# Four more stretches of a hand-written order of instructions (around steps 21–31, 99–104, 127–132 and 160–170 of a decoder layer)

## The chip, the cores and the metric

The kernel runs on one core of one Trainium2 chip. The metric is the device time of one execution in microseconds (us); the time before is 1079.78 us, the median of three runs (1078.62, 1079.78, 1080.32).

## The reference, cut to what matters

One layer on 512 tokens of width 1024, everything in float32: a SwiGLU feed-forward block (inner width 2816), a mixing block (chunked gMLP gating beside a Mamba-2 scan), a second SwiGLU block, a gated embedding and a last RMSNorm.

```python
h = h + 0.5 * swiglu(rmsnorm(h, ffn1_norm[i]), ffn1_w_gate[i], ffn1_w_up[i], ffn1_w_down[i])
n = rmsnorm(h, mix_norm[i])
proj = n @ w_in[i]
u, v, z, xbc, dt_raw = jnp.split(proj, IN_SPLITS, axis=-1)
ya = chunked_spatial_gating(gelu(u), gelu(v), gm_ln_g[i], gm_ln_b[i], gm_w_s[i], gm_b_s[i])   # layernorm of v inside
ya = rmsnorm(ya, gm_out_norm[i])
yb = mamba2_mixer(z, xbc, dt_raw, ...)
h = h + jnp.concatenate([ya, yb], axis=-1) @ w_out[i]
h = h + 0.5 * swiglu(rmsnorm(h, ffn2_norm[i]), ffn2_w_gate[i], ffn2_w_up[i], ffn2_w_down[i])
h = h + sigmoid(rmsnorm(h, ple_norm[i]) @ ple_w_gate[i] + ple_b_gate[i]) * (p[i] @ ple_w_proj[i])
return rmsnorm(h, final_norm)
```

## The kernel before

Every float32 operand of a large product is split into a high part that TensorE can take (`hi`, a cast on ScalarE) and the rest (`lo`, a subtraction on VectorE), and three products are added in PSUM (hi·hi, hi·lo, lo·hi). So every block of weights of 128 x 1024 that arrives by DMA (tile `raw`, `rawb`, `rawd` or `s`) needs one cast (L511, tiles `whi` or `whix`) and one subtraction (L515, tiles `wlo` or `wlox`) before TensorE can use it. `whi` and `wlo` have three buffers each, `whix` and `wlox` one each.

The program is a list of 251 **steps**: 0–99 the embedding product and the first feed-forward block, 100–136 the mixing block, 137–152 the output projection, 153–250 the second feed-forward block. A step has one product on TensorE and pieces around it: `load` (the DMA), `cast` and `split` (L511, L515), `after` (what reads the finished product), `post` and `rest` (more of the same). In the feed-forward blocks a group of 256 inner columns takes seven products (seven instead of eight, by Strassen's scheme, L725; tiles `mm` and `a` in PSUM, inputs `xfa` and `xfb`), and "down" steps (L235, tile `sm`) stand in between; their result is added to the residual `h` by L930. The gate `g` of a group is put together on VectorE (L867, L872, L878, L883), passed through silu on ScalarE (L874) and split again (L894 `ghi`, L896 `glo`).

At the end of the first block the residual tiles are finished two by two (L930), split for the mixing block (L210 on ScalarE and L211 on VectorE, both write tiles `x`) and squared (L277 on ScalarE, tile `tmp`), and GpSimd adds up the squares (L278). In the mixing block, per pair of heads, L1497 and L1461 on VectorE prepare what the scan's products L1471 and L1478 read, L1488 and L1489 take them up, and GpSimd goes on with L1490 and L1491. The layernorm of `v` stands there too: `v_moments` (four `bn_stats`, L1598), `v_factor` (four `bn_aggr`, L1602, and the eleven small instructions of `rsqrt`, L244 to L249) and `v_normed` (L1607). `spatial` sums a weight matrix by a product with ones (L1565), whose two inputs are the tiles `convin`: a cast (L202) and a subtraction (L203). L1569 uses the sum.

The order of the instructions is written out, not found by a scheduler: inside `tc.manual_schedule` TensorE, ScalarE, VectorE and the sync engine's DMA queue take their instructions in the order in which the program makes them. `run` first lists all pieces of all steps in a standing order as generators (`tasks`), each of which yields between its instructions. Then it walks the string `ENTRY`: `split26` runs all that is left of a piece, `split26:1` runs it up to its first yield. What the string does not name follows in the standing order.

```python
for entry in order.split():
    name, _, count = entry.partition(":")
    for _ in islice(tasks[name], int(count) if count else None):
        pass
for task in tasks.values():
    for _ in task:
        pass
```

Of the kernel before, what the change touches and what calls it, by code (L numbers as in the profile page):

```python
# [57 lines left out]
split10 split10.1 load15 product9 split11 after8 load16 product10 after9 split12 load17 after10  # L58
after10.1:1 product11 after11 split13 split14:1 after10.1 split14 product12 after+10 after11.1
after11.2 after12:1 product13 after+11 split15 after13:1 split16 after13:1 after12 product14  # L60
after13
"""

BUFS = {
# [35 lines left out]
def layer_kernel(ctx: ExitStack, tc: tile.TileContext, a: dict, out: bass.AP):  # L100
# [22 lines left out]
    def open_region(side, name):  # L123
        close_region(side)
        names[side] = name
        region[side] = tc.alloc_tile_pool(name=name, bufs=1, side=side, reuse_waits="tile")
        if side == "left":
            pad(region[side], name)
# [279 lines left out]
    def run(steps, opened, order):  # L408

        n = len(steps)  # L410
        held, tasks = [], {}

        def pieces(fn):
            got = fn()
            if isinstance(got, GeneratorType):
                yield from got
            yield

        def do(i, what, which=0):
            if 0 <= i < n:  # L420
                fns = getattr(steps[i], what)
                if what == "after":
                    fns = fns[which] if len(fns) > which else ()
                for k, fn in enumerate(fns if isinstance(fns, (list, tuple)) else [fn for fn in (fns,) if fn]):
                    tasks[f"{what}{'+' * which}{i}" + (f".{k}" if k else "")] = pieces(fn)

        loaded = 0
        for i in range(-3, n + 2):
            while loaded < n and loaded - steps[loaded].lead <= max(i, -1):
                if steps[loaded].from_right and any(i <= k < loaded for k in opened):  # L430
                    held.append(loaded)
                else:
                    do(loaded, "load")
                loaded += 1
            do(i, "product")
            if i in opened:
                tasks[f"open{i}"] = pieces(lambda i=i: open_region("right", opened[i]))
                while held:
                    do(held.pop(0), "load")
            late = 0 <= i - 1 < n and not steps[i - 1].urgent  # L440
            do(i + 2, "cast")
            do(i - 2, "after", 1)
            for what in ("split", "after") if late else ("after", "split"):
                if what == "split":
                    do(i + 2, "split")
                    do(i + 3, "sums")
                else:
                    do(i - 1, "after")
            do(i - 1, "post")
            do(i, "rest")  # L450
        for entry in order.split():
            name, _, count = entry.partition(":")
            for _ in islice(tasks[name], int(count) if count else None):
                pass
# [3 lines that stand above are left out]
# [1278 lines left out]
    with tc.manual_schedule(engines=ORDERED):  # L1736
        run(sum(parts, []) + steps, {ends[0]: "mix_right", ends[2]: "ffn2_right"}, ENTRY)
# [193 lines left out]
```

## Time and profile before

| what | value |
|---|---|
| runs | 1078.62, 1079.78, 1080.32 us |
| the profiled execution | 1078.85 us, of which the profiled span is 1077.1 us |
| TensorE (PE) busy | 1065.2 us, 99% of the span; weight loads (PEld) 992.3 us, 92% |
| VectorE (DVE) busy | 780.1 us, 72% |
| ScalarE (ACT) busy | 514.8 us, 48% |
| GpSimd (POOL) busy | 136.2 us, 13% |
| mean granted TensorE clock | 0.998 |

Times in rows of the profile are microseconds from the start of the span. A row of the timeline gives start, duration, engine, line, operation, names (out<-in), shapes and how many instructions were merged; in brackets stands the idle time of the engine before it and what ended it. Matmuls are pipelined: a row lists a matmul of 256 columns with 0.28 us, but they start 0.113 us apart when nothing is late (24 in 2.72 us), and those of 512 columns 0.227 us. So a wait of TensorE is read here from start to start. The chain of waits is followed back from the last instruction; its rows give start, length, engine, tile, line and count.

### The profile page before, as it was taken

The numbers are of one execution on the slowest core, as the hardware profiler recorded it, in microseconds if no ns is written. First come the engines' busy times: TensorE is split into PE (matmuls) and PEld (weight loads), VectorE is DVE, ScalarE is ACT, GpSimd is POOL, SyncE is SP. The second block draws the span as 40 slices with busy tenths as digits, with TensorE's granted clock in tenths as the row PEclk, the third lists the DMA queues.
The fourth block names the chain that finished last, engine by engine and source line by source line (L and its number), as shares of the span: only waits on it lengthen the run. The fifth ranks groups of instructions, "written<-read, shape, count | busy, mean of one in ns | idle before, by whom it ended". The sixth has DMA issues, their size and how long they took to land.

```text
span 1077.1 us, 18907 instructions
## 1 busy us (share of the span) xinstructions
PE 1065.2 (99%) x7850; PEld 992.3 (92%) x7850; DVE 780.1 (72%) x1081; ACT 514.8 (48%) x711; POOL 136.2 (13%) x125
## 2 busy tenths in 40 slices
PE   9999999999999999999999999999999999999997
PEld 8999999999999888787888888999999999999996
DVE  7987676666666686766997756688766676677766
ACT  6744444343444455575754334354444434343554
POOL 0100000000001201043233000000000000000311
PEclk9999999999999999999999999999999999999999
DMA  9986776665523232444432223667756676633412
GB/s 343 303 226 193 191 192 180 174 184 156 134 60 127 90 98 81 146 131 135 131 105 79 98 98 117 202 162 204 212 142 172 182 195 178 179 115 111 144 41 79
DMA packets 50038, 163.91 MB, mean 152 GB/s; under 512 B 5664, under 2 KB 6176, under 8 KB 49952
## 3 DMA queue, kind: packets, MB, share of 16 engines
q1 hardware_dynamic: 40016, 129.09, 34.4%
q0 software_dynamic: 8640, 31.46, 16.4%
q10 hardware_dynamic: 1296, 2.16, 0.6%
q8 instruction: 61, 1.00, 0.4%
q14 instruction: 25, 0.20, 0.1%
HBM read 158.43 MB, written 4.26 MB: 151 GB/s over the span
## 4 chain that ended last, share of the span: by engine, by line
PE 90%; DVE 4%; DMA 2%; ACT 2%; issue 1%; SPq 0%; DVEq 0%; ACTq 0%
PE sm L235 24%; PE mm L725 20%; PE a L725 15%; PE mm L219 6%; PE sm L219 6%; PE mm L235 6%; PE a L219 5%; PE a L235 3%; PE sm L814 2%; DMA whix<-in_x_rows 1%; PE mm L814 1%; PE a L814 1%; DVE wlo L515 1%; DMA raw<-in_ffn_gu 1%; PE sm L288 1%
## 5 line engine op out<-in xcount | busy, mean ns | idle before, releaser
L511 ACT CAST whi<-raw 128x1024 fp32r<-128x1024 f32 x138 | 144.3, 1046 | 160.6 <-issue 61.0
L515 DVE TENSOR_TENSOR wlo<-raw,whi 128x1024 fp32r<-128x1024 f32 x137 | 172.0, 1255 | 62.4 <-ACT whi L511 60.8
L725 PE MATMUL mm<-xfb,whi 128*128 128x256 f32 x960 | 166.2, 276 | 0.0
L235 PE MATMUL sm<-ghi,wlox 128*128 128x256 f32 x592 | 150.9, 277 | 0.3 <-DVE wlox L515 0.3
L235 PE MATMUL sm<-glo,whix 128*128 128x256 f32 (+1 forms) x512 | 151.1, 295 | 0.0
L235 PE MATMUL sm<-ghi,whix 128*128 128x256 f32 (+1 forms) x512 | 150.3, 294 | 0.0
L725 PEld LDWEIGHTS mm<-xfb,whi 128*128 128x128 f32 x960 | 144.6, 188 | 0.0
L725 PE MATMUL mm<-xfb,wlo 128*128 128x256 f32 x480 | 132.5, 276 | 0.0
L235 PEld LDWEIGHTS sm<-ghi,wlox 128*128 128x128 f32 x592 | 111.1, 188 | 7.5 <-DVE wlox L515 0.7
L725 PE MATMUL a<-xfb,whi 128*128 128x256 f32 x640 | 111.0, 276 | 0.0
L725 PEld LDWEIGHTS a<-xfb,whi 128*128 128x128 f32 x640 | 96.4, 188 | 0.2 <-issue 0.2
L235 PEld LDWEIGHTS sm<-ghi,whix 128*128 128x128 f32 x512 | 96.1, 188 | 0.0
L235 PEld LDWEIGHTS sm<-glo,whix 128*128 128x128 f32 x512 | 96.1, 188 | 0.0
L725 PEld LDWEIGHTS mm<-xfb,wlo 128*128 128x128 f32 x480 | 90.1, 188 | 0.0
L725 PE MATMUL a<-xfb,wlo 128*128 128x256 f32 x320 | 88.5, 276 | 0.0
L515 DVE TENSOR_TENSOR wlox<-rawd,whix 128x1024 fp32r<-128x1024 f32 (+1 forms) x40 | 45.7, 1142 | 58.2 <-ACT whix L511 58.2
L515 DVE TENSOR_TENSOR wlo<-rawb,whi 128x1024 fp32r<-128x1024 f32 x52 | 63.6, 1223 | 18.8 <-ACT whi L511 18.8
L874 ACT ACTIVATE g<-g 128x512 f32<-128x512 f32 x40 | 25.3, 632 | 106.8 <-DVE g L872 106.8
L740 POOL DMA_DIRECT2D raw<-in_ffn_gu x20 | 17.3, 866 | 418.0 <-DVE h L930 195.4
L511 ACT CAST whi<-rawb 128x1024 fp32r<-128x1024 f32 x52 | 54.3, 1044 | 27.2 <-DVE rawb L735 17.8
L930 DVE SCALAR_TENSOR_TENSOR h<-sm,h 128x512 f32<-128x512 f32 x96 | 63.2, 684 | 3.3 <-PE sm L235 3.2
L219 PE MATMUL sm<-x,whi 128*128 128x512 f32 x208 | 65.5, 396 | 0.0
(403 smaller groups left out, 2490.3 us busy)
## 6 DMA issues: line engine op xcount, KB each, us to landing
raw<-in_ffn_gu SPq DMA_DIRECT2D x56, 512.0 KB, 6.2
rawd<-in_ffn_down SPq DMA_DIRECT2D x40, 512.0 KB, 4.2
rawb<-in_ffn_gu SPq DMA_DIRECT2D x32, 512.0 KB, 5.6
raw<-in_ffn_gu POOLq DMA_DIRECT2D x30, 512.0 KB, 5.3
raw<-in_w_in SPq DMA_DIRECT2D x29, 512.0 KB, 3.5
s<-in_ffn_gu SPq DMA_DIRECT2D x20, 512.0 KB, 7.1
s<-in_ffn_gu POOLq DMA_DIRECT2D x20, 512.0 KB, 8.4
raw<-in_w_out SPq DMA_DIRECT2D x16, 512.0 KB, 3.4
```

Of the source, the lines that this page charges most:

```text
L219: nc.tensor.matmul(ps, w, x, start=first and n == 0, stop=last and n == 2, skip_group_check=True)
L235: nc.tensor.matmul(ps[:, tok], wt[:, c], xt[:, tok], start=first and k == i == 0, stop=last and k == len(xs) - 1 and i == len(by_part) - 1 ...
L288: nc.tensor.matmul(ps[:, c : c + 1], part[:, c * P : (c + 1) * P], ones[:, 0:1], start=part is t, stop=part is not t or more is None,)
L511: nc.scalar.copy(self.hi[:, : self.n], self.raw[:, : self.n])
L515: nc.vector.tensor_tensor(self.lo[:, :n], self.raw[:, :n], self.hi[:, :n].bitcast(F32), ALU.subtract)
L725: nc.tensor.matmul(o, wt[:, c], xt, start=fresh and p == m == n == 0, stop=last and n == 2, skip_group_check=True,)
L740: nc.gpsimd.dma_start(w21.raw, self.src[0], accum_op=ALU.add)
L814: nc.tensor.matmul(by_half(ps)[:, s], (whi, whi, wlo)[n][:, c], t[:, s, n % 2], start=not lower and p == i == 0, stop=lower and p == len(s ...
L874: nc.scalar.activation(t, t, AF.Silu)
L930: nc.vector.scalar_tensor_tensor(h[d], ps[d], 0.5, h[d], ALU.mult, ALU.add)
```

## The change

The string `ENTRY` gets more entries, and `run` a rule for them: `..after23` runs all pieces that stand ahead of `after23` in the standing order. Nothing else changes; the lines of the kernel after move by 11 in the head of the file and by 18 behind `run`.

```diff
-after13
+after13 ..after23 split26:1 after23:2 split26 after23 ..product99 after98:1 product99 open99
+cast101 after+97 split101 after98 after+98 after98 load104 product100 cast102 ..load131 load131
+after126.3 load131 product127 cast129 after126 after126.1 after126.2 after126.3 split129 post126
...
         for entry in order.split():
+            if entry.startswith(".."):
+                for name, task in tasks.items():
+                    if name == entry[2:]:
+                        break
+                    for _ in task:
+                        pass
+                continue
             name, _, count = entry.partition(":")
```

TensorE, GpSimd and the sync engine's queue keep their order word for word. VectorE and ScalarE have the same instructions in another order at five points. Two of them are small. In step 23's `after` the cast and subtraction of a down step's weights (`whix` on ScalarE, `wlox` on VectorE) come to stand ahead of the cast and subtraction of the gate (`ghi`, `glo`); before they stood behind them. And in step 126's `after` the four `bn_stats` of `v` come to stand ahead of L1497 and the two L1461 on VectorE, not behind them. The other three are shown by their instructions.

**The start of the mixing block (steps 99 to 102).** On ScalarE, the program before has there (`whi` of `raw_4036` is the cast for step 102, `tmp` are squares of the residual, `x` the split residual):

```order
L511 CAST whi_4156<-raw_3973 128x1024
L277 ACTIVATE tmp_4159<-h_96 128x512
L277 ACTIVATE tmp_4162<-h_100 128x512
L210 ACTIVATE x_4168<-h_97,vec_70 128x512
L210 ACTIVATE x_4172<-h_101,vec_70 128x512
L511 CAST whi_4197<-raw_4036 128x1024
L277 ACTIVATE tmp_4200<-h_97 128x512
L277 ACTIVATE tmp_4203<-h_101 128x512
L210 ACTIVATE x_4209<-h_98,vec_70 128x512
```

and the changed one, same engine, same place:

```order
L529 CAST whi_4157<-raw_3973 128x1024
L288 ACTIVATE tmp_4160<-h_96 128x512
L288 ACTIVATE tmp_4163<-h_100 128x512
L221 ACTIVATE x_4168<-h_97,vec_70 128x512
L221 ACTIVATE x_4172<-h_101,vec_70 128x512
L288 ACTIVATE tmp_4176<-h_97 128x512
L288 ACTIVATE tmp_4179<-h_101 128x512
L529 CAST whi_4203<-raw_4036 128x1024
L221 ACTIVATE x_4209<-h_98,vec_70 128x512
```

The cast for step 102 moved behind the two squares. On VectorE, at the same place, one residual sum (`h_97`) moved ahead of the subtraction for step 101; before:

```order
L211 SCALAR_TENSOR_TENSOR x_4100<-h_100,vec_70,x_4099 128x512
L515 TENSOR_TENSOR wlo_4157<-raw_3973,whi_4156 128x1024
L930 SCALAR_TENSOR_TENSOR h_97<-sm_4038,h_97 128x512
L930 SCALAR_TENSOR_TENSOR h_101<-sm_4061,h_101 128x512
L211 SCALAR_TENSOR_TENSOR x_4169<-h_97,vec_70,x_4168 128x512
```

and now:

```order
L222 SCALAR_TENSOR_TENSOR x_4100<-h_100,vec_70,x_4099 128x512
L948 SCALAR_TENSOR_TENSOR h_97<-sm_4038,h_97 128x512
L533 TENSOR_TENSOR wlo_4158<-raw_3973,whi_4157 128x1024
L948 SCALAR_TENSOR_TENSOR h_101<-sm_4061,h_101 128x512
L222 SCALAR_TENSOR_TENSOR x_4169<-h_97,vec_70,x_4168 128x512
```

So `h_97` no longer stands behind a subtraction that needs the cast of step 101.

**The layernorm of `v` (steps 129 and 130).** On VectorE, before; `convin_5887` is the second input of the product L1565 behind step 130, and `v_factor` begins with the first BN_AGGR:

```order
L1489 TENSOR_TENSOR u_5637<-u_5637,a_818_5834 128x384
L203 TENSOR_TENSOR convin_5887<-xs_5783,convin_5886 128x512
L1632 TENSOR_TENSOR u_5900<-mm_5789,rall_4343 128x512
L515 TENSOR_TENSOR wlo_5880<-raw_5725,whi_5879 128x1024
L1569 SCALAR_TENSOR_TENSOR xs_5699<-sm_5849,vec_70,xs_5699 128x128 x4
L1602 BN_AGGR vstat_120<-bnst_5163 128x2
```

and in the changed program:

```order
L1507 TENSOR_TENSOR u_5637<-u_5637,a_818_5834 128x384
L1620 BN_AGGR vstat_120<-bnst_5163 128x2
...
L255 TENSOR_SCALAR nv_5890<-vstat_120 128x4
L256 TENSOR_SCALAR ny_5891<-nv_5890 128x4
L258 TENSOR_TENSOR nt_5892<-ny_5891 128x4
...
L260 SCALAR_TENSOR_TENSOR vr_121<-nt_5892,ny_5891 128x4
L214 TENSOR_TENSOR convin_5905<-xs_5783,convin_5904 128x512
L1650 TENSOR_TENSOR u_5918<-mm_5789,rall_4343 128x512
```

The whole of `v_factor`, fifteen instructions, now stands directly behind L1489 (L1507 there), and `convin`, L1632, `wlo` and the four L1569 follow it.

**The start of the second feed-forward block (steps 160 to 170).** On VectorE before; `wlo_7459` belongs to the last product of group 1, `wlo_7487` and `wlo_7520` to the first two of group 2, `wlox_7559` to a down step and `wlo_7592` to the third product of group 2:

```order
L515 TENSOR_TENSOR wlo_7459<-rawb_6944,whi_7458 128x1024
L930 SCALAR_TENSOR_TENSOR h_95<-sm_7402,h_95 128x512
L930 SCALAR_TENSOR_TENSOR h_99<-sm_7413,h_99 128x512
L515 TENSOR_TENSOR wlo_7487<-raw_1052_7332,whi_7486 128x1024
L867 TENSOR_TENSOR g_7429<-a_1038_7217,p_1048_7313 128x512
...
L930 SCALAR_TENSOR_TENSOR h_100<-sm_7475,h_100 128x512
L883 TENSOR_TENSOR g_7429<-g_7429,a_1038_7217 128x512
L896 TENSOR_TENSOR glo_7555<-g_7429,ghi_7554 128x1024
L515 TENSOR_TENSOR wlox_7559<-rawd_7400,whix_7558 128x512
L735 TENSOR_TENSOR raw_1052_7332<-raw_1052_7332,s_1056_7365 128x1024
L515 TENSOR_TENSOR wlo_7592<-raw_1052_7332,whi_7591 128x1024
```

and now:

```order
L948 SCALAR_TENSOR_TENSOR h_95<-sm_7402,h_95 128x512
L948 SCALAR_TENSOR_TENSOR h_99<-sm_7413,h_99 128x512
L885 TENSOR_TENSOR g_7429<-a_1038_7217,p_1048_7313 128x512
L533 TENSOR_TENSOR wlo_7487<-raw_1052_7332,whi_7486 128x1024
...
L753 TENSOR_TENSOR raw_1052_7332<-raw_1052_7332,s_1058_7368 128x1024
L901 TENSOR_TENSOR g_7429<-g_7429,a_1038_7217 128x512
L533 TENSOR_TENSOR wlox_7527<-rawd_7400,whix_7526 128x512
L948 SCALAR_TENSOR_TENSOR h_100<-sm_7475,h_100 128x512
L533 TENSOR_TENSOR wlo_7532<-raw_1052_7332,whi_7531 128x1024
L914 TENSOR_TENSOR glo_7564<-g_7429,ghi_7563 128x1024
```

The reading of `a` (L867) moved ahead of a subtraction, and the sum of two weight blocks (L735, L753 in the changed file) with the subtraction that follows from it moved ahead of the gate's `glo`. On ScalarE the casts moved in the same way: that of `s` ahead of the copy L857, that of `rawb` ahead of one silu, those of `rawd` and of the summed block ahead of `ghi`.

More of the change, by code (lines that the diff above doesn't have):

```diff
@@ L60 @@
 after11.2 after12:1 product13 after+11 split15 after13:1 split16 after13:1 after12 product14
-after13
+after13 ..after23 split26:1 after23:2 split26 after23 ..product99 after98:1 product99 open99
+cast101 after+97 split101 after98 after+98 after98 load104 product100 cast102 ..load131 load131
+after126.3 load131 product127 cast129 after126 after126.1 after126.2 after126.3 split129 post126
+post126.1 post126.2 post126.3 rest127 load132 product128 cast130 after127 after127.1 after127.2
+after127.3 split130 post127 post127.1 load133 product129 cast131 after128 after128.1 after128.2
+after128.3 split131 post128 rest129 rest129.1 load134 product130 cast132 after129 post129.1
+after129.1 after129.2 after129.3 split132 post129 ..load167 split163:1 load167 product161
+after160 split163 load168 product162 split164 after161 after161.1:1 split165 after161.1
+product163 after+161 split165 after162 product164 after+162 split166:1 after163 split166
+after163 after163.1 after163.2 product165 after+163 split167 after164:1 sums169 after165:1
+split168 after164 split169:2 after164 load172 product166 after+164 after165 split168 sums169
+load173 product167 after166
 """
```

## The prediction

> **What bounds the kernel now.** The page first: of what the chain that ended last is made.
>
> ```profile
> PE 90%; DVE 4%; DMA 2%; ACT 2%; issue 1%; SPq 0%; DVEq 0%; ACTq 0%
> ```
>
> TensorE sets the time, and the change leaves its order alone. So it can win only what TensorE waits at the moved places, and lose only by a new wait. Next the chain of waits at the start of the second feed-forward block, which also gives the measure.
>
> ```profile
> 716.89 2.72 PE mm L725 x24
> ...
> 725.08 2.75 PE sm L235 x20
> ...
> 727.87 3.06 PE a L725 x24
> ...
> 742.41 2.72 PE mm L725 x24
> ```
>
> When nothing is late a step takes 8.19 / 3 = 2.73 us (716.89 to 725.08 are three steps): 0.113 us a matmul of 256 columns, 0.227 one of 512. From 725.08 to 742.41 stand six such steps and 17.33 us; six times 2.73 is 16.38. At steps 160 to 170 TensorE thus loses **0.95 us**. The same count elsewhere, on TensorE's timeline:
>
> ```profile
> 94.53 0.40 PE L235 MATMUL sm<-glo,whix 128*128 128x512 f32 x1
> 95.23 0.51 PE L235 MATMUL sm<-ghi,wlox 128*128 128x256 f32 x2 [0.30 <-DVE wlox L515]
> 95.58 0.28 PE L235 MATMUL sm<-ghi,whix 128*128 128x256 f32 x1
> ...
> 348.29 0.28 PE L235 MATMUL sm<-ghi,wlo 128*128 128x256 f32 x1
> 348.85 0.47 PE L235 MATMUL sm<-ghi,whi 128*128 128x512 f32 x1 [0.29 <-DVE h L930]
> ...
> 351.75 0.62 PE L219 MATMUL mm<-x,whi 128*128 128x512 f32 x2
> ...
> 356.51 0.39 PE L219 MATMUL mm<-x,whi 128*128 128x512 f32 x1
> 357.20 0.50 PE L219 MATMUL mm<-x,whi 128*128 128x512 f32 x1 [0.30 <-DVE x L211]
> 357.54 0.39 PE L219 MATMUL mm<-x,wlo 128*128 128x512 f32 x1
> ...
> 541.86 0.95 PE L1471 MATMUL sm<-u,yb 128*64 128x128 f32 x13 [0.68 <-DVE u L1461]
> ```
>
> From 94.53 to 95.58 one wide and two narrow matmuls take 1.05 us in place of 0.45: **0.60** lost. From 348.29 to 351.75 are 21 narrow and two wide ones, 3.46 in place of 2.83: **0.63**. From 356.51 to 357.54 two wide ones, 1.03 in place of 0.45: **0.58**. What could be won at these four waits is 0.60 + 0.63 + 0.58 + 0.95 = 2.76 us. The wait at 541.86 is a fifth, near moved instructions.
>
> The brackets show less: 0.30 + 0.29 + 0.30 at three of the four, none at the fourth. The Trainium skill, Perfetto Trace Analysis, section "Identifying the Most-Contended Engine", says that matmul busy time is a bad measure because matmuls are pipelined; by the brackets alone the sum would be 0.9 us, and the starts above side with the page.
>
> **Part 1, step 23.** What TensorE waits for at 95.23 is `wlox`:
>
> ```profile
> 92.82 1.23 DVE L896 TENSOR_TENSOR glo<-g,ghi 128x1024 fp32r<-128x1024 f32 x1 [1.12 <-ACT ghi L894]
> 93.96 1.22 DVE L515 TENSOR_TENSOR wlox<-rawd,whix 128x1024 fp32r<-128x1024 f32 x1
> ...
> 91.73 1.05 ACT L894 CAST ghi<-g 128x1024 fp32r<-128x1024 f32 x1 [3.87 <-DVE g L883]
> ...
> L486 SPq DMA_DIRECT2D rawd<-in_ffn_down x1: 328/328/328, 77.4 to 77.4; - x1
> DMA to landing us min/median/max: 5.5/5.5/5.5
> ```
>
> ScalarE is idle for 3.87 us ahead of `ghi`, and `rawd` has been there since 82.9. With `whix` put ahead, it is cast in that gap, `wlox` runs from 91.7 to 92.9 in VectorE's own gap of 1.12 us, and `glo` starts at 92.9 as now. Behind both nothing is later. TensorE wants `wlox` at 94.76, so all 0.60 go. If the gap were not there, `glo` would be 1.2 us later, which no product reads for several steps.
>
> **Part 2, steps 99 to 102.** The bank that TensorE wants at 348.85 is freed by L930 of `h_97`, which stands behind a subtraction that waits for a cast:
>
> ```profile
> 342.26 1.41 DVE L211 SCALAR_TENSOR_TENSOR x<-h,vec,x 128x512 fp32r<-128x512 f32 x2 [0.20 <-ACT x L210]
> ...
> 354.64 2.50 DVE L211 SCALAR_TENSOR_TENSOR x<-h,vec,x 128x512 fp32r<-128x512 f32 x2 [0.20 <-ACT x L210]
> ...
> 351.87 1.05 ACT L511 CAST whi<-raw 128x1024 fp32r<-128x1024 f32 x1 [1.80 <-issue]
> 352.83 1.15 ACT L277 ACTIVATE tmp<-h 128x512 f32<-128x512 f32 x2
> 353.89 1.34 ACT L210 ACTIVATE x<-h,vec 128x512 fp32r<-128x512 f32 x2
> ...
> 353.60 3.00 POOL L278 TENSOR_TENSOR ssum<-ssum,tmp 128x512 f32<-128x512 f32 x2 [2.97 <-ACT tmp L277]
> ```
>
> The product that `h_97` adds was complete two steps before, at 343.1 (two times 2.73 us and 0.28 of the last matmul, back from 348.29); put ahead of the subtraction, the sum follows the L211 of 342.26 and is done by 344.3. The first wait (0.63) goes, and the cast at 351.87 comes 0.63 earlier too. The two squares (1.15) fit into the 1.80 of idleness ahead of that cast. So the two L210 no longer wait for the squares, only for their `h`: they start near 353.65 and 354.25 in place of 353.89 and 354.52. The last L211, which TensorE waits for at 357.20, takes long because of GpSimd: two such instructions take 1.41 us alone (342.26) and 2.50 here, under the two sums of 353.60. With the squares earlier, those sums end near 354.3, and the last L211 near 355.85; TensorE, 0.63 earlier, wants it at 356.11. The margin is 0.26 us. I take the whole 0.58; if one more sum of GpSimd falls on L211, none of it (bounds 0 to 0.58).
>
> **Part 3, steps 126 to 131.** First the four `bn_stats` ahead of L1461:
>
> ```profile
> 524.50 2.46 DVE L1598 BATCH_NORM_STATS2 bnst<-ya 128x6 f32<-128x512 f32 x4
> ...
> 527.95 1.09 PE L1471 MATMUL a<-u,yb 128*64 128x128 f32 x16
> ```
>
> L1461 and these change places, so L1461 now ends where they ended, at 527.0; TensorE reads it at 527.95. That costs nothing, with 0.8 us to spare. Nothing in it shortens the work up to 541.86, where VectorE is late without a gap; I leave that wait as it is.
>
> Then `v_factor`, which moves from 549.14 to 545.53, right behind L1489:
>
> ```profile
> 549.14 0.41 DVE L1602 BATCH_NORM_AGGREGATE vstat<-bnst 128x2 f32<-128x12 f32 x4
> ...
> 545.70 1.40 POOL L1490 TENSOR_TENSOR xs<-xs,u 128x384 f32<-128x384 f32 x1 [3.48 <-DVE u L1489]
> ...
> 551.15 1.30 POOL L278 TENSOR_TENSOR ssum<-ssum,tmp 128x512 f32<-128x512 f32 x1 [1.82 <-ACT tmp L277]
> ...
> 549.53 0.63 PE L1565 MATMUL sm<-convin,onesr 128*128 128x512 f32 x2
> ...
> 541.73 0.14 issue
> ...
> 516.26 1.01 POOL L1490 TENSOR_TENSOR xs<-xs,u 128x384 f32<-128x384 f32 x1 [4.69 <-DVE u L1489]
> 517.34 1.31 POOL L1491 TENSOR_TENSOR xs<-xs,tmp 128x512 f32<-128x512 f32 x1
> ...
> 517.52 1.15 DVE L248 SCALAR_TENSOR_TENSOR nt<-nt,nv 128x4 f32<-128x4 f32 x1
> ...
> 519.88 0.16 DVE L249 SCALAR_TENSOR_TENSOR rtok<-nt,ny 128x4 f32<-128x4 f32 x1
> ```
>
> L1489, which ends at 545.61, also sets off GpSimd's L1490 and then L1491. The eleven small instructions of such a factor stood under these two once before: one of 0.16 us took 1.15, up to the end of L1491, and the last of the eleven ended 3.8 us after L1490 had begun (516.26 to 520.04). Here L1490 begins at 545.70 and holds them up to 546.7, L1491 to 548.1 (1.01 and 1.31 us). Three of them are through by then, the other eight need 0.2 each: 549.7. Then `convin` (0.68, as another subtraction of its size) ends at 550.3, and TensorE goes on 0.14 later, which is the time from L1461 to TensorE at 541.73: 550.44. It wants the tile 0.23 after 549.53, at 549.76. That is a **new wait** of 0.68, and 0.1 of slow start as behind the others: **0.8 us**. Bounds: without GpSimd's sums the eleven end at 548.2, and nothing waits; if they last into the third sum at 551.15, the wait is near 4.0. I take 0.8, by the rows of 516 to 520.
>
> The Trainium skill, SBUF — State Buffer, section "Who interferes with whom", says that a VectorE instruction with two inputs in SBUF and a GpSimd one that reads SBUF exclude each other for a whole instruction, whoever starts first. With a shared bandwidth in its place, at half speed under the sums, the eleven would end near 549.2 and the new wait be 0.2. The 1.15 that ends with L1491 speaks for the page.
>
> What follows is 0.2 us later on VectorE and 0.8 on TensorE, so no second wait comes of it.
>
> **Part 4, steps 160 to 170.** The two waits are for L867 (TensorE may not add into `a` before it is read) and for the summed block's `wlo`:
>
> ```profile
> 727.04 0.68 DVE L867 TENSOR_TENSOR g<-a,p 128x512 f32<-128x512 f32 x1
> 738.35 1.23 DVE L515 TENSOR_TENSOR wlo<-raw,whi 128x1024 fp32r<-128x1024 f32 x1 [1.17 <-ACT whi L511]
> ...
> 702.45 0.86 POOL L743 DMA_DIRECT2D s<-in_ffn_gu  x1 [0.19 <-issue]
> ```
>
> L867 needs a product that is complete near 725.2 (the step ends at 725.08), and now runs there, almost two microseconds before TensorE's 727.8. The summed block's sum now stands some 5 us earlier, and its subtraction comes near 734.0 to 735.2 in place of 738.35 to 739.58; TensorE, 0.95 earlier, reads it near 738.7. The DMA of what is summed was issued at 702.45, so the earlier sum does not wait for it and hold up what stands behind it on VectorE, `wlox` above all. `glo` is later for it, by 2 us, and read several steps on. All 0.95 go.
>
> **The sum.** −0.60 − 0.63 − 0.58 − 0.95 + 0.8 = −1.96, say −2.0 us. The profiled execution took 1078.85 (span 1077.1, and 1.75 around it); it lies 0.93 below the median 1079.78. Against the median: **1077.8 us**. About 0.2%, 2.2 us, is what a measurement of this kernel can tell from no change, and the forecast lies just inside.
>
> **The rivals.**
> - *GpSimd does not hold up `v_factor`, or not long enough.* Then the new wait is missing: −2.8, 1077.0 us. For it: margin 0.7 us only. Against it: 517.52. Should the wait at 541.86 go as well, 1076.1.
> - *A won place does not pay:* part 2's second half, with its margin of 0.26, or half of part 4. Then −1.2, 1078.6 us.
> - *Slower: `v_factor` lasts into GpSimd's third sum.* L278 begins at 551.15. If the small instructions are not done by then, they lose a third turn of 1.3 us, `convin` ends near 553.6 and TensorE waits 4.0: 4.0 − 2.76 is +1.3, 1081.1 us, and above 1082 if a won place fails too. It decides once `convin` ends after 552.4. Against it: 1.4 us of room between 549.7 and 551.15.
> - *TensorE's gain is eaten, and the change does nothing,* 1079.8: later work would have to hang on something fixed in time. Against it: the chain is 90% TensorE.
>
> **How the numbers follow.** Chances: forecast 0.47, no new wait 0.24, a won place fails 0.15, slower 0.09, nothing 0.05. Faster by over 0.2% (below 1077.6): just under half of the forecast, nearly all of the second case: 0.45. Slower by over 0.2%: the worse part of the fourth case and what no row shows, 0.08. Within: 0.47. The range runs from the second case's lower end, 1075.9, over the third to just short of the fourth, 1080.2.
>
> **What would show it.** On TensorE's timeline the waits near 95, 348, 357, 727 and 739 are gone, and that for L1461 is still there; a new one of some 0.7 us stands at the second L1565, released by `convin`; on VectorE two small instructions of `v_factor` take about 0.7 and 1.2 us. Wrong it would be if the waits at the feed-forward places only move to another tile, or if L1565 waits for microseconds.

## The result and the profile after

The changed kernel takes **1076.63 us** (median of ten runs, 1076.33 to 1076.95). Over ten runs the kernel before has a median of 1078.9 us (1078.07 to 1080.32). The ratio is 0.9977, with a 95% interval from 0.9968 to 0.9987: faster by 0.23%. Forecast were 1077.8 us, in a range from 1075.9 to 1080.2.

The profiled execution of the changed kernel took 1076.37 us, its span is 1074.7 (1077.1 before). The page's chain of waits, by engine:

```profile
PE 93%; DVE 4%; ACT 2%; DMA 1%; issue 0%; SPq 0%; DVEq 0%; ACTq 0%
```

TensorE's share of the chain rose from 90% to 93%, some 31 us, but that is no measure of the change. The chain no longer leaves TensorE near 86 to 95 and 343 to 357 (22 us), and leaves it for 11 us more around `v_factor`; the other 20 us lie ahead of 29, where nothing was moved and the chain went through DMAs in one execution and through TensorE in the other. TensorE's timeline of the changed kernel shows the places themselves, read from start to start as before:

```profile
94.31 0.40 PE L246 MATMUL sm<-glo,whix 128*128 128x512 f32 x1
94.54 0.39 PE L246 MATMUL sm<-ghi,wlox 128*128 128x256 f32 x2
94.77 0.28 PE L246 MATMUL sm<-ghi,whix 128*128 128x256 f32 x1
...
347.47 0.28 PE L246 MATMUL sm<-ghi,wlo 128*128 128x256 f32 x1
347.59 0.39 PE L246 MATMUL sm<-ghi,whi 128*128 128x512 f32 x1
...
350.32 0.63 PE L230 MATMUL mm<-x,whi 128*128 128x512 f32 x2
...
355.09 0.62 PE L230 MATMUL mm<-x,whi 128*128 128x512 f32 x2
355.55 0.39 PE L230 MATMUL mm<-x,wlo 128*128 128x512 f32 x1
...
539.83 0.95 PE L1489 MATMUL sm<-u,yb 128*64 128x128 f32 x13 [0.71 <-DVE u L1479]
...
547.52 0.40 PE L1583 MATMUL sm<-convin,onesr 128*128 128x512 f32 x1
548.33 0.51 PE L1583 MATMUL sm<-convin,onesr 128*128 128x512 f32 x1 [0.41 <-DVE convin L214]
548.67 0.63 PE L230 MATMUL mm<-x,whi 128*128 128x512 f32 x2
```

The same stretches as in the prediction, before and now: at step 26 one wide and two narrow matmuls take 0.46 us (94.31 to 94.77) in place of 1.05; the last 21 narrow and two wide ones of step 99 take 2.85 (347.47 to 350.32) in place of 3.46; two wide ones in the mixing block take 0.46 (355.09 to 355.55) in place of 1.03. The two matmuls of 355.09 now stand in one row: between them there is no hole any more. The wait for L1479 (L1461 before) is still there, with 0.71 in the bracket where 0.68 stood. And a new one came: the second L1583 starts 0.81 after the first where 0.23 would do, 0.58 too late, and the next matmul follows 0.34 after that, 0.11 too late. The chain at the second feed-forward block:

```profile
723.75 2.75 PE sm L246 x20
...
740.12 2.72 PE mm L743 x24
```

These are the same six steps as 725.08 to 742.41 before. They take 16.37 us in place of 17.33.

So the five places together give −0.59 − 0.61 − 0.57 − 0.96 + 0.69 = **−2.04 us**. The other 0.4 of the difference of the two spans (2.4) lies where nothing was moved, about half of it in the first 50 us and half behind 1000 us; the last section comes back to such differences.

### The profile page after: what moved, and what is told of

Same layout as the page of the kernel before. It is cut to its first block, busy times and chain, and to the rows that moved or that the text cites. A ratio compares the mean times of both kernels' runs of the same rounds, so it can differ in the third digit from the quotient of the medians.

```text
span 1074.7 us, 18908 instructions
## 1 busy us (share of the span) xinstructions
PE 1063.3 (99%) x7850; PEld 991.4 (92%) x7850; DVE 779.3 (73%) x1081; ACT 515.1 (48%) x711; POOL 135.8 (13%) x125
## 4 chain that ended last, share of the span: by engine, by line
PE 93%; DVE 4%; ACT 2%; DMA 1%; issue 0%; SPq 0%; DVEq 0%; ACTq 0%
PE sm L246 24%; PE mm L743 20%; PE a L743 15%; PE mm L230 6%; PE mm L246 6%; PE sm L230 5%; PE a L230 5%; PE a L246 3%; PE sm L832 2%; PE mm L832 1%; PE a L832 1%; PE sm L1661 1%; DMA g<-in_p 1%; PE sm L299 0%; DVE tmp L1773 0%; PE sm L1425 0%
## 5 line engine op out<-in xcount | busy, mean ns | idle before, releaser
L246 PE MATMUL sm<-glo,whix 128*128 128x256 f32 (+1 forms) x512 | 151.1, 295 | 0.0
L246 PE MATMUL sm<-ghi,wlox 128*128 128x256 f32 x592 | 150.8, 277 | 0.0
L246 PE MATMUL sm<-ghi,whix 128*128 128x256 f32 (+1 forms) x512 | 150.3, 294 | 0.0
L246 PEld LDWEIGHTS sm<-ghi,wlox 128*128 128x128 f32 x592 | 111.2, 188 | 6.8
L246 PEld LDWEIGHTS sm<-glo,whix 128*128 128x128 f32 x512 | 96.1, 188 | 0.0
L246 PEld LDWEIGHTS sm<-ghi,whix 128*128 128x128 f32 x512 | 96.1, 188 | 0.0
L230 PE MATMUL sm<-x,whi 128*128 128x512 f32 x208 | 65.5, 396 | 0.0
```

Of the source, the lines that this page charges most:

```text
L230: nc.tensor.matmul(ps, w, x, start=first and n == 0, stop=last and n == 2, skip_group_check=True)
L246: nc.tensor.matmul(ps[:, tok], wt[:, c], xt[:, tok], start=first and k == i == 0, stop=last and k == len(xs) - 1 and i == len(by_part) - 1 ...
```

## Experiments

Theory A is that of the prediction: every wait of TensorE is won or lost at its own place, the places add up, and v_factor costs what it does because GpSimd's sums hold up its small instructions. Each rival is named with the run that could have shown it. Edits are given against the changed kernel, whose line numbers they keep (with GpSimd's two sums left out, what stands behind them is one line lower). Times are medians of five or more runs where a ratio stands beside them; otherwise there is one run (these four took 1076.73 to 1077.31 us), and the trace decides.

### v_factor put back

```diff
-after129 post129.1 after129.1 after129.2 after129.3 split132 post129
+after129 after129.1 after129.2 after129.3 split132 post129 post129.1
```

> The changed kernel with only v_factor put back behind convin, L1650, wlo and the four L1587. Theory A (each wait is won or lost at its own place; v_factor costs what TensorE waits for convin at the second L1583, 0.58 us and a little slow start): that wait goes, nothing else moves, so 0.6 us below the changed kernel, about 1076.0 beside 1076.6, and 2.8 below the kernel before. Rival B (the time before the end is fixed by something else, so that a wait removed in the middle comes back later): the wait goes and the time stays within 0.2 of the changed kernel's.

1076.01 us (1075.89 to 1076.17), ratio to before 0.9970 (0.9959 to 0.9982). TensorE's timeline at the two L1583:

```profile
547.54 0.63 PE L1583 MATMUL sm<-convin,onesr 128*128 128x512 f32 x2
```

Both stand in one row again, and the wait is gone. The median falls by 0.6 us, the whole of it; the intervals of the two ratios overlap, so the place in the trace decides. In the chain, a row of 48 matmuls of L230 starts at 366.50 in the changed kernel and at 366.52 here, and far behind, near the end, a row of 172 of L246, first in the changed kernel, then here:

```profile
993.53 21.89 PE sm L246 x172
```

```profile
992.88 21.89 PE sm L246 x172
```

Between the two rows lie 627.03 us in the changed kernel and 626.36 here, 0.67 less. A wait that is removed in the middle does not come back later; rival B falls.

### The same fifteen instructions, ahead of GpSimd's sums

```diff
-after129 post129.1 after129.1 after129.2 after129.3 split132 post129
+post129.1 after129 after129.1 after129.2 after129.3 split132 post129
```

> The changed kernel with v_factor one place further ahead, before L1506 and L1507 and not behind them: the same fifteen instructions stand ahead of convin, but GpSimd's two sums, which L1507 sets off, now begin when v_factor is through. Theory A (GpSimd's sums hold the small instructions up): v_factor takes 2.6 us without a hole, convin ends near 546.9 on the changed kernel's time axis, 0.85 before TensorE wants it (547.75), and the wait of 0.58 goes: 0.6 us below the changed kernel. Rival B (fifteen instructions are too many ahead of convin, whatever GpSimd does): the wait stays at 0.5 us or more and the time is the changed kernel's.

1076.06 us, ratio 0.9970 (0.9959 to 0.9982); between the same two rows, 626.36 us. First the changed kernel's VectorE and GpSimd in this stretch, two views:

```profile
543.95 0.76 DVE L255 TENSOR_SCALAR nv<-vstat 128x4 f32<-128x4 f32 x1
...
544.95 1.14 DVE L258 TENSOR_TENSOR nt<-ny 128x4 f32<-128x4 f32 x1
...
547.50 0.16 DVE L260 SCALAR_TENSOR_TENSOR vr<-nt,ny 128x4 f32<-128x4 f32 x1
547.58 0.69 DVE L214 TENSOR_TENSOR convin<-xs,convin 128x512 fp32r<-128x512 f32 x1
```

```profile
543.67 1.02 POOL L1508 TENSOR_TENSOR xs<-xs,u 128x384 f32<-128x384 f32 x1 [3.48 <-DVE u L1507]
544.76 1.30 POOL L1509 TENSOR_TENSOR xs<-xs,tmp 128x512 f32<-128x512 f32 x1
```

Of eleven instructions on four elements each, nine take about 0.16 us. The two others take 0.76 and 1.14, and end at 544.71 and 546.09, each within 0.03 us of the end of a sum of GpSimd (544.69 and 546.06). With v_factor ahead of L1507, which sets the sums off, VectorE shows:

```profile
542.43 0.41 DVE L1620 BATCH_NORM_AGGREGATE vstat<-bnst 128x2 f32<-128x12 f32 x4
...
544.86 0.16 DVE L260 SCALAR_TENSOR_TENSOR vr<-nt,ny 128x4 f32<-128x4 f32 x1
...
546.07 0.69 DVE L214 TENSOR_TENSOR convin<-xs,convin 128x512 fp32r<-128x512 f32 x1
```

From 542.43 to 545.02 are 2.6 us, without a hole, and `convin` ends at 546.76. The first L1583 starts at 547.55 and the second wants it 0.23 later, so there is 1.0 us to spare, and the two stand in one row. The same number of instructions stands ahead of `convin` as in the changed kernel, and nothing waits: it is not the length of the queue.

### GpSimd's two sums left out

```diff
-        nc.gpsimd.tensor_tensor(y[:, P:], y[:, P:], grow[:, P:], ALU.add)
-        nc.gpsimd.tensor_tensor(y, y, mix["z", j], ALU.mult)
+        if j != 6:
+            nc.gpsimd.tensor_tensor(y[:, P:], y[:, P:], grow[:, P:], ALU.add)
+            nc.gpsimd.tensor_tensor(y, y, mix["z", j], ALU.mult)
```

> The changed kernel without GpSimd's two sums of step 129 (the product of state and decay, and the gate, of one pair of heads are left out of the output). Theory A: v_factor takes 0.41 + 11 x 0.2 = 2.6 us in one piece, convin ends near 546.8, the wait for it (0.58) goes. Rival B (the count of instructions ahead of convin): the wait stays at 0.4 us or more.

VectorE, where v_factor stands as in the changed kernel:

```profile
544.41 0.41 DVE L1621 BATCH_NORM_AGGREGATE vstat<-bnst 128x2 f32<-128x12 f32 x4
...
546.84 0.16 DVE L260 SCALAR_TENSOR_TENSOR vr<-nt,ny 128x4 f32<-128x4 f32 x1
```

Again 2.6 us in one piece, and TensorE has no wait: the two products with ones (L1584 here) stand in one row at 548.40. Between the same two rows as above lie 626.37 us. This and the run before take away the same cost by different means, one by the order, one by the work.

### One more instruction on GpSimd

```diff
-        nc.gpsimd.tensor_tensor(y, y, mix["z", j], ALU.mult)
+        nc.gpsimd.tensor_tensor(y, y, mix["z", j], ALU.mult); j == 6 and nc.gpsimd.tensor_tensor(grow[:, P:], grow[:, P:], grow[:, P:], ALU.mult)
```

> The changed kernel with one more multiplication of 128x384 on GpSimd (a dead tile times itself) behind the two sums of step 129, so that GpSimd is busy for 1.0 us more, up to 547.1. The output stays that of the reference. Theory A (exclusion by whole instructions): one more small instruction of v_factor is held up to the end of the added one, v_factor ends 0.9 to 1.1 us later, and TensorE's wait for convin grows from 0.58 to about 1.6 us. Rival B (v_factor is long by its count alone): the wait stays 0.58. Rival C (VectorE and GpSimd share a bandwidth): the small instructions, of 0.16 us, become some tenths longer each and the wait grows by 0.2 to 0.5 us.

VectorE, GpSimd and TensorE in turn:

```profile
544.28 0.75 DVE L255 TENSOR_SCALAR nv<-vstat 128x4 f32<-128x4 f32 x1
...
545.27 1.15 DVE L258 TENSOR_TENSOR nt<-ny 128x4 f32<-128x4 f32 x1
546.45 0.75 DVE L259 SCALAR_TENSOR_TENSOR nt<-nt,nv 128x4 f32<-128x4 f32 x1
547.23 0.16 DVE L260 SCALAR_TENSOR_TENSOR ny<-nt,ny 128x4 f32<-128x4 f32 x1
```

```profile
546.36 0.82 POOL L1509 TENSOR_TENSOR u<-u 128x384 f32<-128x384 f32 x1
```

```profile
547.82 0.40 PE L1583 MATMUL sm<-convin,onesr 128*128 128x512 f32 x1
549.25 0.51 PE L1583 MATMUL sm<-convin,onesr 128*128 128x512 f32 x1 [1.03 <-DVE convin L214]
```

A third small instruction is held, 0.75 in place of 0.16, to the end of the added one (547.18), and the ones behind it are as short as ever. TensorE's wait grows from 0.58 to 1.20 us (1.43 from start to start), and between the two rows lie 627.67 us, 0.64 more than in the changed kernel. The mechanism is that of theory A: whole instructions, one for each of GpSimd's. Its number was too large (1.6), since the added instruction took 0.82 us and not 1.0, and the held one would have taken 0.16 anyway. A shared bandwidth, rival C, would have made several instructions a little longer; only one became long.

### The third stretch alone

All else as before.

> Of the four stretches only the one around steps 127 to 132 (the bn_stats and v_factor moved), all else as before. Theory A (the places add up): 0.6 to 0.7 us above the kernel before, with the one new wait for convin, and the other four waits of TensorE as before. Rival B (the new wait came only because TensorE was 1.9 us earlier there): no new wait and the time of before, within 0.2 us.

1079.72 us, ratio 1.0004 (0.9995 to 1.0013): by its time not to be told from no change. TensorE's timeline tells more:

```profile
550.11 0.40 PE L1583 MATMUL sm<-convin,onesr 128*128 128x512 f32 x1
550.95 0.50 PE L1583 MATMUL sm<-convin,onesr 128*128 128x512 f32 x1 [0.44 <-DVE convin L214]
```

The second L1583 is 0.61 too late, with TensorE not ahead of its old time: the wait belongs to this stretch alone, and rival B falls.

### The fourth stretch alone

> Of the four stretches only the one around steps 160 to 170, all else as before. Theory A: six steps from the second down step on take 16.4 us and not 17.33, so 0.95 us below the kernel before. Rival B (only the two waits themselves, 0.20 + 0.20, are won, since the slower beat of the matmuls between them has another cause): 0.4 us.

1077.79 us beside 1078.77, ratio 0.9992 (0.9983 to 1.0001). The chain:

```profile
725.08 2.75 PE sm L246 x20
...
730.55 5.44 PE mm L743 x48
...
741.46 2.72 PE mm L743 x24
```

Six steps take 16.38 us, 0.95 less than before. From start to start the two waits themselves were 0.20 and 0.20, so more than half of the gain was the slower beat of the matmuls behind each wait: these 48 took 5.65 in the kernel before. It went with the wait, against rival B; why matmuls are slower behind a wait, no run here shows.

### The first piece alone, and the second stretch alone

> Of the four stretches only the first piece (whix and wlox of step 26 ahead of ghi and glo), all else as before. Theory A: the wait for wlox near 95 goes and the others stay: 0.6 to 0.8 us below the kernel before. Rival B: this wait stands in for the arrival of weights, which differs from one execution to the next, and comes back within the first 100 us at another tile: less than 0.3 us below.

> Of the four stretches only that around steps 99 to 104 (h_97 ahead of a subtraction, two squares ahead of a cast), all else as before. Theory A (the places add up): the waits near 348 and 357 go, 1.2 us below the kernel before. Rival B: the second went in the changed kernel only because of the first piece's 0.6 us, and here its margin of 0.26 us fails: 0.6 us below.

The first piece alone: 1078.16 us, ratio 0.9993 (0.9984 to 1.0002). The second stretch alone: 1077.44, ratio 0.9989 (0.998 to 0.9997). In the traces the waits near 95 and those near 348 and 357 are gone, each in its own kernel, and the rest is there. For the first piece the time alone does not decide between 0.6 and less than 0.3; the trace, in which the wait for `wlox` is gone and no other has come in the first 100 us behind it, speaks for theory A. The second ratio is 1.2 us, as theory A has it. The four parts by their ratios, 0.9993 x 0.9989 x 1.0004 x 0.9992 = 0.9978, come out at the whole, 0.9977. Each ratio is uncertain by 0.0009, about as much as a part is worth, so an agreement this close is partly luck, and it is the places in the traces that carry the claim.

Nor does a place have one price. In the kernel with the second stretch alone, where the first piece is as before, the wait for `wlox` near 95 is longer:

```profile
95.89 0.51 PE L246 MATMUL sm<-ghi,wlox 128*128 128x256 f32 x2 [0.71 <-DVE wlox L533]
```

From the wide matmul ahead of it (94.78) to the third narrow one (96.23) are 1.45 us, so 1.00 is lost, as in the kernel with the third stretch alone (0.99); with the fourth alone it is 0.80, and in the execution of the kernel before 0.60. In the same way the eight steps of the fourth stretch that start at 725.08 took 22.77 in the kernel before and 23.05 in that with the first piece alone, against 21.81 without the waits. What made the difference between these executions was not found.

### Half of the second stretch

The squares put back behind the cast:

```diff
-split101 after98 after+98 after98 load104 product100 cast102
+split101 after98 load104 product100 cast102 after+98
```

> The changed kernel with the two squares (L288) of h_97 and h_101 put back behind the cast for step 102 on ScalarE; the earlier sum h_97 on VectorE stays. Theory A (the second wait of the first place went because the squares, and with them GpSimd's sums, ended before the last L222): the wait near 356 comes back with 0.4 to 0.8 us, the one near 348 stays away. Rival B (the earlier h_97 alone was enough, and the squares' place does not matter): neither comes back.

VectorE's last L222 and TensorE:

```profile
353.33 2.50 DVE L222 SCALAR_TENSOR_TENSOR x<-h,vec,x 128x512 fp32r<-128x512 f32 x2 [0.20 <-ACT x L221]
```

```profile
355.88 0.50 PE L230 MATMUL mm<-x,whi 128*128 128x512 f32 x1 [0.29 <-DVE x L222]
```

The same pair in the changed kernel:

```profile
353.40 1.42 DVE L222 SCALAR_TENSOR_TENSOR x<-h,vec,x 128x512 fp32r<-128x512 f32 x2 [0.19 <-ACT x L221]
```

The pair of L222 takes 2.50 us again, under two sums of GpSimd that run from 352.27 to 355.27, and the second wait is back, 0.45 us; the first stays away. Then the other half, with `h_97` put back behind the subtraction:

```diff
-..product99 after98:1 product99 open99
+..product99 product99 open99
```

> The changed kernel with the sum h_97 put back behind the subtraction for step 101 on VectorE; the two squares stay ahead of the cast on ScalarE. Theory A (two causes, one for each wait): the wait near 348 comes back with 0.4 to 0.5 us, and the one near 356 stays away. Rival B (both waits hang on h_97): both come back.

```profile
347.89 0.47 PE L246 MATMUL sm<-ghi,whi 128*128 128x512 f32 x1 [0.29 <-DVE h L948]
...
355.42 0.50 PE L230 MATMUL mm<-x,whi 128*128 128x512 f32 x1 [0.21 <-DVE x L222]
```

```profile
348.54 3.38 DVE L222 SCALAR_TENSOR_TENSOR x<-h,vec,x 128x512 fp32r<-128x512 f32 x2 [0.20 <-ACT x L221]
351.88 1.33 DVE L1151 TENSOR_TENSOR whi<-raw,whi 128x128 fp32r<-128x128 f32 x1
```

**Both** waits are back (0.45 and 0.37), which theory A did not expect. The last L222 takes 1.42 us here, so it is not held; but the instructions ahead of it are, L1151 for one, with 1.33 us for 128 columns where the changed kernel has 0.52; it ends at 353.22, behind GpSimd's last sum (353.07). With `h_97` late, VectorE falls under one sum more. So the second wait goes only if both edits are made, each of them is needed, and neither suffices.

### Two cures for the wait that stayed

The first cure takes two instructions from ahead of L1479, with v_factor put back:

```diff
-after127.1 after127.2 after127.3 split130 post127 post127.1 load133 product129 cast131 after128 after128.1 after128.2 after128.3
+after127.1 after127.2 post127 post127.1 load133 product129 cast131 after128 after128.1 after128.2 split130 after127.3 after128.3
```

> The changed kernel with v_factor put back, and besides with the subtraction wlo for step 130 and L1650 of u0 moved behind the first convin, so that they no longer stand ahead of L1479 on VectorE. Theory A: without these two instructions (0.60 and 1.22 us) ahead of it, the last L1479 ends 1.3 to 2.3 us earlier than 539.7, and the wait of 0.88 for it, which the change left, goes as well: 0.6 + 0.9 = 1.5 us below the changed kernel, about 1075.1. Rival B: VectorE is late there because of GpSimd, whose sums then fall on other instructions and eat the room: the wait for L1479 stays above 0.5 us. Rival C: wlo is now late for its product near 541.2 and the wait only moves there.

1075.67 us (1074.88 to 1076.55), ratio 0.9966 (0.9953 to 0.9978). The wait near 540 is gone (its 16 matmuls stand in one row, 1.09 us); from the first L1489 to the first L1583 are 1.68 us in place of 2.79, so it had cost 1.11 from start to start, and not only its bracket. But near 554 stands, on TensorE, VectorE and GpSimd:

```profile
553.71 1.49 PE L1489 MATMUL a<-u,yb 128*64 128x128 f32 x15
...
555.89 1.16 PE L1661 MATMUL sm<-xs,ya 128*128 128x128 f32 x8
```

```profile
549.77 1.22 DVE L259 SCALAR_TENSOR_TENSOR nt<-nt,nv 128x4 f32<-128x4 f32 x1
```

```profile
549.68 1.30 POOL L289 TENSOR_TENSOR ssum<-ssum,tmp 128x512 f32<-128x512 f32 x1 [0.74 <-ACT tmp L288]
```

Fifteen of these matmuls take 1.49 us where sixteen took 1.09, and L1661 starts 2.18 behind the first of them where 1.68 did in the changed kernel: a new wait of 0.50 from start to start (0.28, as the next expectation has it, is too little). TensorE comes 1.1 us earlier to what the next L1479 makes, and v_factor ahead of it is held by the third sum. No rival had this place. The second kernel adds the place of v_factor from the second experiment:

> The changed kernel with v_factor ahead of L1506 and L1507, and with wlo for step 130 and L1650 of u0 behind the first convin: both cures together. Theory A: the wait for L1479 near 540 (0.87) and that for convin near 548 (0.58) go, and the one of 0.28 near 554, which came of v_factor standing late and being held by GpSimd's third sum, does not come: 1.45 us below the changed kernel, about 1075.2, and 3.7 to 4.1 below the kernel before. Rival B: GpSimd's third sum now falls on L1479 instead, which needed 2.38 us in this order where it takes 1.28 alone, and TensorE, 0.9 earlier, waits for it near 554 with 0.3 us or more.

1075.36 us (1074.79 to 1075.89), ratio 0.9967 (0.9955 to 0.998): 3.6 us below the kernel before, with an interval that does not exclude the 3.7 to 4.1 expected, and no more than the kernel above. The trace shows what failed. L1479 does take 2.38 us, as rival B has it, but TensorE does not wait for it. It waits for `convin` once more:

```profile
547.31 0.50 PE L1583 MATMUL sm<-convin,onesr 128*128 128x512 f32 x1 [0.33 <-DVE convin L214]
```

That is 0.50 us too late: the two instructions moved behind the first `convin` now stand ahead of the second, and TensorE wants it 1.1 earlier. Both theories failed here: theory A had no wait left, rival B had it at another place. VectorE has no gap between 530 and 555, but for one of 1.25 us ahead of a `yb`; in such a stretch another order moves a wait by one place and wins only a part of it. Against the changed kernel both medians are lower, by 1.0 and 1.3 us, with intervals of the ratios that overlap its own; between the rows near 366 and 993 their traces take 1.24 and 1.18 us less. Which of the two is better their runs do not decide.

## Why the prediction was right

**What bounds the kernel, and the measure.** Right. The starts of matmuls gave 2.76 us at the four places; measured were 0.59 + 0.61 + 0.57 + 0.96 = 2.73. By the brackets alone it would have been 0.9. The four parts, each run alone, changed the waits of their own places and left the others standing.

**Part 1** was right: −0.60 forecast, −0.59 measured. The mechanism is the forecast one: `wlox` now runs ahead of `glo`,

```profile
91.33 1.22 DVE L533 TENSOR_TENSOR wlox<-rawd,whix 128x1024 fp32r<-128x1024 f32 x1
```

which with 0.29 us added is 91.62 to 92.84 (forecast 91.7 to 92.9). That the size agrees so well has some luck in it: forecast and measurement rest on the same execution of the kernel before, and in those of three kernels that keep this place as it was the wait was 0.80 to 1.00.

**Part 2** was right in its sum, −0.63 and −0.58 forecast, −0.61 and −0.57 measured. The chain of reasons held too, with 0.81 us added to the times of the changed kernel (its L222 of 341.45 is the L211 of 342.26): GpSimd's sums end at 354.05 (forecast 354.3), the last L222 at 355.63 (355.85). What the prediction said too loosely is that the first edit gives one wait and the second edit the other. The second wait needs both.

**Part 3** had the right mechanism. The `bn_stats` cost nothing; the wait for L1461 stayed. With 2.03 us added (L1508 at 543.67 is the L1490 of 545.70), v_factor ends at 549.69 (forecast 549.7) and `convin` at 550.30 (550.3); the two long instructions took 0.76 and 1.14 us (0.7 and 1.2). The term was **mis-sized by 0.1**: 0.69 in place of 0.8. TensorE went on 0.06 us after `convin`, not the 0.14 taken from the chain's row behind L1461. That GpSimd's sums are the cause, two runs show, the sums later and the sums away. That whole instructions exclude each other, and no bandwidth is shared, a third shows: with one instruction more on GpSimd one small instruction more was held, and those between stayed at 0.16 us.

**Part 4** was right: −0.95 forecast, −0.96 measured in the whole and 0.95 alone. With 1.33 us added, L867 (L885) ran at 725.11 (forecast 725.2) and the summed block's `wlo` from 733.85 (734.0).

**The sum** was −1.96 and came out at −2.04 at these places; by the medians of ten runs each the difference is −2.27. **The level** was off by 1.2 us, and 0.9 of that is the starting point: the forecast was put on the median of three runs, 1079.78, and ten runs of the same kernel have 1078.9. The profiled execution, 1078.85, on which the terms rest, was the better base, as it turned out. With it the same sum gives 1076.9. The forecast put the change just inside the 0.2% that it held to be within the scatter; measured are 0.23%, just outside, for which it had given 0.45.

**The rivals.** *No new wait* (1077.0) lies nearest to the measured time, but its mechanism is refuted: the wait is there, and is larger when GpSimd does more. *A won place does not pay* did not happen, though half of part 2 would have brought it about. The *slower* case did not come: v_factor was through at 547.66, 1.5 us before the third sum at 549.15, and even with one instruction more on GpSimd at 548.58, 0.9 before it (549.45). *Does nothing* fell with the first experiment.

## What to carry to other kernels

Read the waits of a matmul engine from start to start, price each at its own place, and add them up: where that engine carries the chain, a wait that goes is won to the end, and one that comes is lost to the end. Look at what the engines' neighbours do in the same microsecond before a group of small instructions is moved: here eleven of 0.16 us took 3.7 us in place of 2.1, because two of them were held up to the ends of two large ones. Where VectorE has no gap left, as here around 540, reordering handed part of the wait on to the next place: 1.1 us won and 0.5 given back.

## What the runs showed of the hardware

**The start differs between executions of the same instructions.** Nine of the kernels (the changed one and those made from it) have the same program up to 340 us. The chain of waits gives the start of the same down step near 108 us; the three rows are of the changed kernel, of that with `h_97` put back, and of the first cure:

```profile
107.87 5.47 PE sm L246 x44
```

```profile
107.73 5.47 PE sm L246 x44
```

```profile
108.80 5.47 PE sm L246 x44
```

They lie up to 1.07 us apart, half of what the whole change is worth. In the first cure's execution TensorE waited 0.68 us near 29 for a `wlo`, from start to start (0.50 in the bracket), where the other two show 0.03 and 0.07; what made it late was not followed to its cause. Two single executions can't be subtracted as wholes here; the same place in both can, but as the wait for `wlox` shows, the size of a wait near the start is better taken from several.

**A small instruction pays for a large one.** A VectorE instruction on four elements took up to 1.30 us (v_factor put back, L258) when a GpSimd instruction with inputs in SBUF ran, also one with a single input in SBUF (L255, 0.76), while the four `bn_aggr` ahead of it, the last two beside the same sum, took no longer than without it (0.41 us together). The Trainium skill, SBUF — State Buffer, section "Who interferes with whom", says that an instruction of VectorE with one input can need the pair of ports that it shares with GpSimd if it runs in a mode with two ports, and names tensor_scalar; L255 is one, and the 0.76 agrees.
